# Input projections by Strassen's scheme, as one phase ahead of the attentions

## The chip, the cores and the metric

The kernel runs on one core of a Trainium2 chip. The metric is the device time of one execution in microseconds, the median over runs. TensorE is called PE in the profile (its weight loads PEld), VectorE DVE, ScalarE ACT, GpSimd POOL, and SyncE, which issues the DMAs, SP.

## What is computed

Two layers of a streaming encoder, for 1024 prompt tokens and for 8 streams of 16 sample tokens with caches. In each layer (shortened from the reference):

```python
h = x @ w_in                                    # 1024 -> 2756 columns, split into 11 parts
(c_q, c_kv, k_rope, g_mla, f_q, f_k, f_v, f_logit, g_fox, m_q, g_mem) = split(h)
q   = rms_norm(c_q) @ w_uq                      # 4 heads x (128 + 64 rotated)
lat = rms_norm(c_kv); kr = rope(k_rope)         # outputs of the kernel as well
logf = log_sigmoid(f_logit + b_f)
o_mla = attend(q, [lat @ w_ukv keys, kr], lat @ w_ukv values)   # chunk-causal, 4 heads x 128
o_fox = attend(f_q, f_k, f_v, cumsum(logf))     # causal, with forgetting, 4 heads x 64
o_mem = attend(m_q, mem @ w_mk, mem @ w_mv)     # 256 memory rows, 4 heads x 64
mixed = [o_mla*silu(g_mla), o_fox*silu(g_fox), o_mem*silu(g_mem)]
y = layer_norm(alpha * x + mixed @ w_out)
```

All is float32. A product is carried in a rounded high part and the rest (hi and lo, type fp32r) of both operands, as three matmuls.

## The kernel before

Every product goes through `mm3` (lines 193 to 195, hi by hi, hi by lo, lo by hi), plain products through `mm` (198) and transposes through `tr` (202). `split` makes hi with a cast on ACT (177, 180) and lo with a subtraction on DVE (178, 181); `wsplit` does it for weights, lo on DVE or POOL (187). The token operand X of a layer is feature-major: four blocks of 256 prompt tokens and one of the 128 sample tokens, each in eight chunks of 128 features.

The input projection is cut into eleven groups of columns. `tokproj` gives a token-major result (tokens on partitions, 128 of them, the group's 302 or 306 columns moving), `featproj` a feature-major one (128 columns on partitions, 256 tokens moving); 24 matmuls each, contracted over 1024 features. The groups are the gates `ge`, `gf`, `gm0`, `gm1` (`gates`, silu at 375), the queries `mq`, `fq0`, `fq1` (`qproj`, 353), keys and values of the fox heads `kv0`, `kv1` (`fox_kv`, 523 to 571) and the low-rank rows `lr0`, `lr1` (`lowrank`).

Order within a layer: `ge`, the memory keys and values (`mem_prep`), `mq`; then the memory attention, then the fox attention in two pairs of heads, then `lowrank` with the row norms and its transposes, the queries Q (`mla_x`), rotated queries (`qrope`), the latent attention and the tail (`w_out`, layer norm). `attn` runs one unit of an attention (scores and softmax of 256 queries of a head) and then the P transposes and P times V of the unit before; between units it takes a step of filler generators. In the memory attention the filler is `kv0` and `gf`, in the fox attention `gm` and the sample streams' attention. So the projections stand between softmax steps of the attentions. In layer 0's tail the output tiles are transposed into layer 1's X as they come, and `mem_prep` of layer 1 runs there.

A scheduler orders each engine's instructions by simulated times and priority of the program order. PSUM has three banks `pss`, two `psx`, two `pst` (transposes) and one `pso` (attention outputs); SBUF pools give `u` 25 slots and `w` 8 slots of 4 KB, `x` 12 of 2 KB.

Of the kernel before, what the change touches and what calls it, by code (L numbers as in the profile page):

```python
# [74 lines left out]
RPOOL = (1, 3, 5, 7)
PRE = 9
JF = (2,3,1,0)
JA = (0,2,1,3)
TURN = (3,7)


class Enc:
# [141 lines left out]
    def xpair(self, tiles, banks=None):  # L224

        out = []
        for kh in range(2):
            hi = self.u([P, 4, 256], F32R, "xh")
            lo = self.u([P, 4, 256], F32R, "xl")
            for kk in range(2):  # L230
                ps = (banks or [self.pst])[kk % len(banks or "1")]()
                v = ps.rearrange("p (k t) -> p k t", k=2)
                for a in range(2):
                    for b in range(2):
                        k = kh * 4 + kk * 2 + a
                        self.tr(v[:, a, b * P:(b + 1) * P], tiles[b][:, k * P:(k + 1) * P])
                self.split(hi[:, kk * 2:kk * 2 + 2, :], lo[:, kk * 2:kk * 2 + 2, :], v)
            out.append((hi, lo))
        return out
# [13 lines left out]
    def xtok(self, X, i, k):  # L253

        if i == 8:
            return tuple(t[:, k, :] for t in X[4])
        return tuple(t[:, k % 4, (i % 2) * P:(i % 2 + 1) * P] for t in X[i // 2][k // 4])


    def wload(self, src, alloc=None):  # L260

        parts, _, kn, n = src.shape
        raws = []
        for a in range(parts):
            raw = (alloc or self.w)([P, kn, n if n <= P or n > 256 else 256], name="raw")
            self.load(raw[:, :, :n], src[a])
            raws.append(raw[:, :, :n])
        return raws

    def wprep(self, src, raws=None, pieces=1):  # L270

        out = []
        for raw in raws or self.wload(src):
            _, kn, n = raw.shape
# [3 lines left out]
            for a in range(0, kn, kn // pieces):  # L278
                k = slice(a, a + kn // pieces)
                self.wsplit(hi[:, k, :n], lo[:, k, :n], raw[:, k])  # L280
# [1351 lines left out]
```

## Time and profile before

| | |
|---|---|
| median of 3 runs | 1437.37 us (1436.32 to 1439.52) |
| the profiled execution's own time | 1439.67 us |
| its span in the trace | 1437.9 us |
| PE busy | 1402.4 us, 98% |
| DVE, ACT, POOL busy | 756.6, 620.8, 515.8 us (53%, 43%, 36%) |
| DMA | 180.64 MB, mean 126 GB/s |
| granted clock, mean over the span | 0.99 |

A row of a group reads: line, engine, operation, output<-inputs, shapes, count, then busy time in us and mean ns of one, then the engine's idle time just before these and what ended it. A row of stages reads: stretch in us, its length, busy time and count on each engine, the clock granted to TensorE, DMA share, GB/s. A timeline row reads: start in us, duration, engine, line, operation. Matmuls overlap in the records, so their pace is the distance of their starts.

### The profile page before, as it was taken

The numbers are of one execution on the slowest core, as the hardware profiler recorded it, in microseconds if no ns is written. First come the engines' busy times: TensorE is split into PE (matmuls) and PEld (weight loads), VectorE is DVE, ScalarE is ACT, GpSimd is POOL, SyncE is SP. The second block draws the span as 40 slices with busy tenths as digits, with TensorE's granted clock in tenths as the row PEclk, the third lists the DMA queues.
The fourth block names the chain that finished last, engine by engine and source line by source line (L and its number), as shares of the span: only waits on it lengthen the run. The fifth ranks groups of instructions, "written<-read, shape, count | busy, mean of one in ns | idle before, by whom it ended". The sixth has DMA issues, their size and how long they took to land.

```text
span 1437.9 us, 27746 instructions
## 1 busy us (share of the span) xinstructions
PE 1402.4 (98%) x10222; PEld 1257.8 (87%) x10222; DVE 756.6 (53%) x1863; ACT 620.8 (43%) x1624; POOL 515.8 (36%) x722
## 2 busy tenths in 40 slices
PE   7999999999999999999999999999999999999997
PEld 6999989989988788888899999899899887887885
DVE  6236555266045665666663365643642565566664
ACT  6344454354255544722233454544533554455100
POOL 0233254354364221712322234434625541235121
PEclk9999999999999999999999999999999999999999
DMA  7223332345254431363541234234443633234531
GB/s 286 91 73 91 113 126 87 124 140 166 83 176 130 133 115 53 132 215 118 181 160 54 85 101 153 78 89 137 142 148 113 203 95 123 96 114 143 165 118 73
DMA packets 142344, 180.64 MB, mean 126 GB/s; under 512 B 32384, under 2 KB 99776, under 8 KB 142208
## 3 DMA queue, kind: packets, MB, share of 16 engines
q1 hardware_dynamic: 142208, 178.86, 38.6%
q8 instruction: 81, 1.33, 0.4%
q14 instruction: 55, 0.45, 0.1%
HBM read 138.69 MB, written 40.12 MB: 124 GB/s over the span
## 4 chain that ended last, share of the span: by engine, by line
PE 87%; DMA 4%; DVE 3%; ACT 2%; POOL 2%; issue 1%; SPq 0%; POOLq 0%; DVEq 0%; ACTq 0%
PE pss L193 15%; PE pss L195 14%; PE pss L194 14%; PE pss L198 10%; PE pso L198 7%; PE pst L202 7%; PE psx L198 6%; PE psx L193 4%; PE psx L195 4%; PE psx L194 4%; DMA memx<-in_mem_t_dram 1%; POOL wl L187 1%; PE psx L202 1%; DMA raw<-in_w_uqn_dram 1%; DMA g<-md 1%
## 5 line engine op out<-in xcount | busy, mean ns | idle before, releaser
L187 POOL TENSOR_TENSOR wl<-raw,wh 128x1024 fp32r<-128x1024 f32 (+3 forms) x40 | 101.6, 2543 | 208.1 <-ACT wh L184 98.1
L178 DVE TENSOR_TENSOR ptw<-pst,ptw 128x512 fp32r<-128x512 f32 (+1 forms) x192 | 122.0, 642 | 55.2 <-ACT ptw L177 53.8
L177 ACT CAST ptw<-pst 128x512 fp32r<-128x512 f32 (+1 forms) x192 | 103.4, 552 | 97.3 <-PE pst L202 88.9
L193 PE MATMUL pss<-wh,xh 128*128 128x306 f32 (+1 forms) x384 | 118.2, 309 | 0.4 <-ACT h L693 0.4
L195 PE MATMUL pss<-wh,xl 128*128 128x306 f32 (+1 forms) x384 | 117.6, 307 | 0.0
L194 PE MATMUL pss<-wl,xh 128*128 128x306 f32 (+1 forms) x384 | 117.5, 307 | 0.0
L193 PE MATMUL psx<-xh,wh 128*128 128x256 f32 x384 | 109.9, 287 | 7.8 <-ACT wh L184 6.7
L193 PE MATMUL pss<-woh,msh 128*128 128x512 f32 x288 | 114.0, 396 | 0.7 <-ACT msh L1251 0.6
L195 PE MATMUL pss<-woh,msl 128*128 128x512 f32 x288 | 114.0, 397 | 0.1
L194 PE MATMUL pss<-wol,msh 128*128 128x512 f32 x288 | 113.6, 394 | 0.0
L193 PE MATMUL pss<-xh,wh 128*128 128x256 f32 x384 | 109.9, 286 | 0.2
L194 PE MATMUL psx<-xl,wh 128*128 128x256 f32 x384 | 109.8, 286 | 0.0
L195 PE MATMUL psx<-xh,wl 128*128 128x256 f32 x384 | 108.9, 285 | 0.0
L195 PE MATMUL pss<-xh,wl 128*128 128x256 f32 x384 | 108.4, 282 | 0.0
L194 PE MATMUL pss<-xl,wh 128*128 128x256 f32 x384 | 108.3, 282 | 0.0
L396 POOL TENSOR_SCALAR pa<-pa,col 128x128 f32<-128x128 f32 (+3 forms) x64 | 47.7, 750 | 109.4 <-DVE col L395 62.0
L193 PEld LDWEIGHTS psx<-xh,wh 128*128 128x128 f32 x384 | 73.6, 192 | 8.5 <-ACT wh L184 6.7
L198 PE MATMUL pso<-ptw,vh 128*128 128x256 f32 (+1 forms) x336 | 73.7, 296 | 2.3 <-DVE ptw L178 1.3
L193 PEld LDWEIGHTS pss<-xh,wh 128*128 128x128 f32 x384 | 72.5, 189 | 2.9 <-DVE col L431 1.5
L184 ACT CAST wh<-raw 128x1024 fp32r<-128x1024 f32 (+4 forms) x52 | 54.8, 1057 | 45.7 <-PE pss L194 14.4
L193 PEld LDWEIGHTS pss<-wh,xh 128*128 128x128 f32 x384 | 72.4, 189 | 2.2 <-ACT h L693 1.8
L195 PEld LDWEIGHTS pss<-wh,xl 128*128 128x128 f32 x384 | 72.3, 189 | 1.6 <-issue 1.6
(364 smaller groups left out, 4198.9 us busy)
## 6 DMA issues: line engine op xcount, KB each, us to landing
gd<-gg SPq DMA_DIRECT2D x64, 128.0 KB
kT<-in_fox_kt_dram SPq DMA_DIRECT2D x32, 256.0 KB
vraw<-in_fox_v_dram SPq DMA_DIRECT2D x32, 256.0 KB
kT<-in_mla_kt_dram SPq DMA_DIRECT2D x32, 256.0 KB
vraw<-in_mla_v_dram SPq DMA_DIRECT2D x32, 256.0 KB
raw<-in_w_out_dram SPq DMA_DIRECT2D x16, 512.0 KB
g<-md SPq DMA_DIRECT2D x16, 512.0 KB
raw<-in_w_lr_dram SPq DMA_DIRECT2D x8, 612.0 KB
```

Of the source, the lines that this page charges most:

```text
L177: nc.scalar.copy(hi, ps)
L178: nc.vector.tensor_tensor(lo, ps, self.f(hi), op=ALU.subtract)
L184: self.nc.scalar.copy(hi, raw)
L187: (self.nc.vector if dve else self.nc.gpsimd).tensor_tensor(lo, raw, self.f(hi), op=ALU.subtract)
L193: self.nc.tensor.matmul(ps, ah, bh, start=first and x == 0, stop=False)
L194: self.nc.tensor.matmul(ps, ah, bl, start=False, stop=False)
L195: self.nc.tensor.matmul(ps, al, bh, start=False, stop=last and x == n - 1)
L198: self.nc.tensor.matmul(ps, lhsT, rhs, start=start, stop=stop)
L202: self.nc.tensor.transpose(out, in_, self.ident[:k, :k])
L396: self.nc.gpsimd.tensor_scalar(p, p, rs, 1.0, op0=ALU.mult, op1=ALU.mult)
```

## The change

`w_in` is regrouped ahead of the launch into eleven pairs of 256 columns (2816, with 60 columns of padding), and the whole projection is made by `project()` before any attention. For each pair, tokens and features are each cut in halves and the pair's two chunks of 128 columns are the third split, so that a pair is a 2x2 block product; seven products (Winograd's form, each 12 matmuls of 128x512, into three banks `pss` and two `psx`) take the place of eight. For that, sums of token blocks (`xprep`) are made once per layer, sums of weight blocks (`wsums`) per pair, and sums of the products after it (`u2`, `u3`, `v`, `cout`). The sample tokens take 24 ordinary matmuls of 128x256 per pair (`part`).

```diff
+    def xprep(self, r):                      # operands s1..s4 and 22, per layer
+        for k in range(4):
+            t1, t2 = self.pe(), self.pe()
+            dve.tensor_tensor(t1, r["21"][k], r["22"][k], op=ALU.add)
+            dve.tensor_tensor(t2, t1, r["11"][k], op=ALU.subtract)
+            self.xone(s1, k, t1, dve)        # xone: hi by ACT, lo by the engine named
...
+            pool.tensor_tensor(t4, r["12"][k], t2, op=ALU.subtract)
+            self.xone(s2, k, t2, dve)
...
+            pool.tensor_tensor(t3, r["11"][k], r["21"][k], op=ALU.subtract)
+            self.xone(s3, k, t3, dve)
+            self.xone(s4, k, t4, dve)
+            self.xone(a22, k, r["22"][k], pool)
...
+    def wbase(self, raw):
+        h, l = self.pw([P, 4, 256], F32R, "wh"), self.pw([P, 4, 256], F32R, "wl")
+        self.nc.scalar.copy(h, raw)
+        self.nc.gpsimd.tensor_tensor(l, raw, self.f(h), op=ALU.subtract)
...
+    def wsums(self, raws):
...
+        def one(a, b, op=ALU.subtract):
+            r = self.x([P, 4, P], name="tr")
+            dve.tensor_tensor(r, a, b, op=op)
+            t = self.w([P, 2, 4, P], F32R, "wt")
+            self.nc.scalar.copy(t[:, 0], r)
+            dve.tensor_tensor(t[:, 1], r, self.f(t[:, 0]), op=ALU.subtract)
...
+    def project(self, l, X, XS):
...
+        for n, name in enumerate(PAIRS):
...
+            prod(a, cols(B0, 0), "11")
+            p1 = self.pe()
+            nc.scalar.copy(p1, a)
...
+            part(sm, B0, 0)
+            part(sm, B1, 1)
...
+            prod(a, cols(B1, 0), "12")
+            self.cout(name, 0, 0, a, p1)
...
+            prod(d, T[0], "s1")
...
+            prod(b, T[1], "s2")
+            u2 = self.pe()
+            nc.vector.tensor_tensor(u2, b, p1, op=ALU.add)
+            v = self.x([P, 512], name="co")
+            nc.gpsimd.tensor_tensor(v, u2, p5, op=ALU.add)
...
+            prod(c, T[2], "s3")
+            u3 = self.pe()
+            nc.vector.tensor_tensor(u3, c, u2, op=ALU.add)
+            self.cout(name, 1, 1, p5, u3)
...
+            prod(d, cols(B1, 1), "s4")
+            self.cout(name, 1, 0, d, v, v)
...
+            prod(c, T[3], "22")
+            self.cout(name, 0, 1, c, u3)
```

All results are feature-major and go to DRAM: gates, after their silu on 128x512 tiles, to `gd` as before, the rest to fourteen chunks `cd`. The attentions reload them: `qhead` (mem and fox query heads, 128x1024), `fox_kv` (keys doubled on the partitions, values by transposes), `early_rows` (rotary key and forget logits, by transposes) and `lowrank`. The norms of the prompt's low-rank rows are now over partitions:

```diff
+            nc.scalar.activation(q, t, AF.Square)                 # 5 chunks of 128x1024
...
+            for c in (slice(0, 512), slice(512, D)):
+                ps = self.psw()
+                self.mm(ps, self.ones, q[:, c])
+                nc.vector.tensor_scalar(r[:, c], ps, 1.0 / n, EPS, op0=ALU.mult, op1=ALU.add)
+                nc.gpsimd.tensor_tensor(r[:, c], r[:, c], self.mhalf.broadcast_to([P, 512]), op=ALU.pow)
...
+            nc.vector.scalar_tensor_tensor(t, t, self.ng[:, c:c + 1], rs[0 if kv else 1], op0=ALU.mult, op1=ALU.mult)
...
+            hi, lo = self.u([P, D], F32R, "lrh"), self.u([P, D], F32R, "lrl")
+            nc.scalar.copy(hi, t)
+            nc.gpsimd.tensor_tensor(lo, t, self.f(hi), op=ALU.subtract)
```

The filler of the memory and fox attentions is now `proj()`: `fox_kv`, Q of the four heads, `qrope`, the first V and K of the latent attention; the sample streams run beside both. `mem_prep` of layer 1 is no longer in layer 0's tail. The tail takes its tiles in the order 0 to 5, 8, 6, 7, and behind tile 7 comes `xprep` of layer 1. Pools: `u` 30 slots, `w` 4. The outputs `p_lat`, `p_fk` and `p_fv` are written feature-major and turned round after the launch.

How it moves instructions. POOL, from the memory values to the memory attention's softmax, before (`mv` are memory values, `wl` weight rests, `pm` the memory softmax's rows):

```order
L338 TENSOR_TENSOR mv_335<-st_485,mv_335 128x4x64
L187 TENSOR_TENSOR wl_671<-raw_664,wh_670 128x1024
L187 TENSOR_TENSOR wl_971<-raw_966,wh_970 128x1224
L509 TENSOR_SCALAR pm_952<-pm_952,col_962 128x256 x2
L509 TENSOR_SCALAR pm_1027<-pm_1027,col_1037 128x256 x2
```

and after (`rs` are the norms' factors, `lrl` the rests of the normed low-rank rows):

```order
L499 TENSOR_TENSOR mv_2393<-st_2571,mv_2393 128x4x64
...
L851 TENSOR_TENSOR rs_2640<-rs_2640,mhalf 128x512 x2
...
L851 TENSOR_TENSOR rs_2658<-rs_2658,mhalf 128x512 x2
...
L862 TENSOR_TENSOR lrl_2791<-lr_2365,lrh_2790 128x1024
L862 TENSOR_TENSOR lrl_2797<-lr_2367,lrh_2796 128x1024
...
L862 TENSOR_TENSOR lrl_2802<-lr_2369,lrh_2801 128x1024
...
L862 TENSOR_TENSOR lrl_2807<-lr_2371,lrh_2806 128x1024
L746 TENSOR_TENSOR lex_2743<-lex_2743,lf_2722 128x4
L862 TENSOR_TENSOR lrl_2812<-lr_2373,lrh_2811 128x1024
L643 TENSOR_SCALAR pm_2816<-pm_2816,col_2826 128x256 x2
```

The powers and the subtractions of the low-rank rows, which stood behind the attentions, are now in POOL's queue ahead of the first scaling of a memory softmax row. DVE at the same place, after (`lr` are the low-rank rows, `pss` under `TENSOR_REDUCE` the memory scores):

```order
L850 TENSOR_SCALAR rs_2658<-pss_2663 128x512
...
L857 SCALAR_TENSOR_TENSOR lr_2365<-lr_2365,ng_297,rs_2640 128x1024
L857 SCALAR_TENSOR_TENSOR lr_2367<-lr_2367,ng_297,rs_2640 128x1024
L857 SCALAR_TENSOR_TENSOR lr_2369<-lr_2369,ng_297,rs_2658 128x1024
...
L637 TENSOR_REDUCE col_2817<-pss_2815 128x2
L641 RECIPROCAL col_2826<-col_2818 128x2
L666 TENSOR_TENSOR fkl_2999<-fkr_2995,fkh_2998 128x1024
```

The products of the norms stand ahead of the first maximum of memory scores. PE in the memory attention, before (`kd` doubled fox keys, `wh_970` weights of `kv0`, `ptw` split P tiles):

```order
L194 MATMUL psx_1407<-wl_971,xh_492 128x306
L198 MATMUL pso_1226<-ptw_1232,mv_334 64x256
L198 MATMUL pso_1226<-ptw_1232,mv_335 64x256
L198 MATMUL pso_1226<-ptw_1232,mv_335 128x256
L202 MATMUL pst_1299<-ident,pm_1173 128x128 x4
L195 MATMUL psx_1407<-wh_970,xl_493 128x306
L193 MATMUL psx_1407<-wh_970,xh_492 128x306
```

and after:

```order
L187 MATMUL pst_2875<-ident,pm_2816 128x128 x4
L183 MATMUL pss_3148<-mkh_2389,q_2493 128x256
L183 MATMUL pss_3148<-mkl_2391,q_2493 128x256
...
L187 MATMUL pst_2915<-ident,pm_2837 128x128 x4
L183 MATMUL pso_2874<-ptw_2880,mv_2392 128x256
L187 MATMUL psx_3368<-ident,spr_3290 128x128 x2
L183 MATMUL pso_2874<-ptw_2880,mv_2392 64x256
L183 MATMUL pso_2874<-ptw_2880,mv_2393 64x256
```

Between two P transposes there stood projection matmuls on tokens X; now scores and sample work stand there.

More of the change, by code (lines that the diff above doesn't have):

```diff
@@ L221, in late_consts, with xop @@
         self.load(self.sin, self.i["k_sin"])
[L224 to L239, printed above, removed]
+    def xop(self):
+        return [(self.u([P, 2, 512], F32R, "xh"), self.u([P, 2, 512], F32R, "xl")) for _ in range(2)]
@@ L251, in xsample @@
         return hi, lo
[L253 to L267, printed above, removed]
-        return raws
@@ L284, in tokproj, with wraw @@
[L284 to L289 removed]
+    def wraw(self, l, n):
+        raws = [self.ptw([P, 4, 256], F32, "raw") for _ in range(2)]
+        for a in range(2):
+            self.load(raws[a], self.i["w_pairs"][l, n, a])
+        return raws
@@ L292, in mem_prep, with wprep @@
+    def wprep(self, raws):
+        out = []
+        for raw in raws:
+            hi, lo = self.w(raw.shape, F32R, "wh"), self.w(raw.shape, F32R, "wl")
+            self.wsplit(hi, lo, raw)
+            out += [(hi[:, k], lo[:, k]) for k in range(raw.shape[1])]
+        return out
     def mem_prep(self, l):
@@ L301, in mem_prep, with raws @@
                 M.append((hi, lo))
-        alloc = lambda shape, name: self.ptw(shape, F32, name)
-        raws = self.wload(self.i["w_mk"][l], alloc)
+        def raws(src):
+            out = []
+            for a in range(2):
+                raw = self.ptw([P, 4, 256], F32, "raw")
+                self.load(raw, src[a])
+                out.append(raw)
+            return out
+        W = self.wprep(raws(self.i["w_mk"][l]))
         yield
@@ new lines, in fox_kv @@
+        K = []
+        for e in range(2):
+            t = self.w([P, D], name="fkr")
+            self.twice(6 + p, e, t)
+            hi, lo = self.u([P, D], F32R, "fkh"), self.u([P, D], F32R, "fkl")
+            nc.scalar.copy(hi, t)
+            nc.vector.tensor_tensor(lo, t, self.f(hi), op=ALU.subtract)
+            K.append((hi, lo))
+            yield
+        t = self.u([P, D], name="fvr")
+        self.load(t, self.cd[8 + p])
+        V = [self.x([P, 2, 2, P], F32R, "fv") for _ in range(4)]
@@ L570, in fox_kv @@
+        for g in range(2):
+            pt = self.pst()
+            for a in range(4):
+                kb = g * 4 + a
+                self.tr(pt[:, a * P:(a + 1) * P], t[:, kb * P:(kb + 1) * P])
+            for b in range(2):
+                src = pt[:, b * 256:b * 256 + 256].rearrange("p (k e d) -> p k e d", k=2, e=2)
+                v = V[g * 2 + b]
+                self.split(v[:, :, :, 0:64], v[:, :, :, 64:128], src)
             yield
-        self.fkv = KH, KL, V
+        self.fkv = K, V
@@ L1257, in tail_start, with tail @@
         return lg, lb, prep
-    def tail(self, WO, start, ready, after, fill, early):
+    def tail(self, WO, start, ready, after, fill):
         nc = self.nc
@@ L1449, in fill @@
                 next(sg, None)
-        if not start:
-            start.extend(self.tail_start(l, xin))
-        self.tail(WO, start, ready, after, fill, early)
+        start.extend(self.tail_start(l, xin))
+        self.tail(WO, start, ready, after, fill)
     def main(self):
@@ L1476, in more @@
[L1476 to L1494 removed]
+        nc = self.nc
```

824 lines of the change are left out of this document (394 added, 430 removed).

## The prediction

> **What bounds the kernel now.** I read the share of each engine and the chain of waits first, then busy time by stage, then the groups of instructions by shape, and last single rows of the timeline for paces.
>
> ```profile
> PE 1402.4 (98%) x10222; PEld 1257.8 (87%) x10222; DVE 756.6 (53%) x1863; ACT 620.8 (43%) x1624; POOL 515.8 (36%) x722
> PE 87%; DMA 4%; DVE 3%; ACT 2%; POOL 2%; issue 1%; SPq 0%; POOLq 0%; DVEq 0%; ACTq 0%
> ```
>
> TensorE is busy 98% of the span and is 87% of the chain, so a matmul taken away is worth its time, as long as nothing new makes TensorE wait. By stage (length, then busy time of PE, PEld, DVE, ACT, POOL, then clock, DMA share, GB/s):
>
> ```profile
> 0.00:10.00 10.00, 3.30 (x15) 3.30 (x16) 4.20 (x7) 5.71 (x9) 0.43 (x6) 1.00 0.80 297
> 10.00:20.00 10.00, 9.71 (x75) 9.51 (x74) 8.75 (x15) 7.71 (x14) 0.00 (x0) 1.00 0.90 336
> 20.00:36.00 16.00, 12.21 (x82) 10.91 (x82) 11.12 (x17) 9.84 (x18) 0.00 (x0) 0.89 0.66 247
> 84.00:175.00 91.00, 88.69 (x692) 86.78 (x691) 46.63 (x112) 45.10 (x134) 31.75 (x50) 0.98 0.34 98
> 175.00:353.00 178.00, 176.67 (x1493) 165.33 (x1491) 94.67 (x277) 87.10 (x219) 89.25 (x126) 1.00 0.42 128
> 353.00:411.00 58.00, 57.51 (x467) 54.71 (x466) 11.29 (x36) 19.75 (x70) 25.20 (x40) 1.00 0.37 114
> 411.00:482.00 71.00, 70.35 (x543) 58.77 (x542) 41.90 (x106) 38.95 (x112) 29.07 (x59) 1.00 0.47 145
> 482.00:614.00 132.00, 130.08 (x873) 106.88 (x872) 80.23 (x237) 68.68 (x182) 47.69 (x46) 1.00 0.33 113
> 614.00:735.00 121.00, 120.34 (x600) 99.84 (x601) 75.16 (x109) 25.77 (x38) 28.03 (x26) 1.00 0.51 174
> 735.00:745.00 10.00, 9.59 (x81) 9.30 (x80) 7.85 (x11) 4.33 (x7) 3.87 (x3) 1.00 0.39 118
> ```
>
> These are layer 0's start, memory attention (84 to 175), fox attention (to 353), low-rank projection (to 411), turns and queries (to 482), latent attention (to 614) and tail; 735 opens layer 1. TensorE waits only in the first 36 us. Elsewhere DVE and POOL are about half busy, and projection matmuls stand between softmax steps as cover.
>
> **Matmuls removed and added.** Pace is the distance of starts, since ends overlap; between each pair of rows are 24 steps.
>
> ```profile
> 757.34 0.28 PE L193 MATMUL psx<-wh,xsh 128*128 128x256 f32 x1
> ...
> 760.17 0.28 PE L193 MATMUL psx<-xh,wh 128*128 128x256 f32 x1
> ...
> 359.72 0.30 PE L193 MATMUL pss<-wh,xh 128*128 128x306 f32 x1
> ...
> 363.12 0.30 PE L193 MATMUL pss<-wh,xh 128*128 128x306 f32 x1
> ...
> 1399.80 0.40 PE L193 MATMUL pss<-woh,msh 128*128 128x512 f32 x1
> ...
> 1405.45 0.40 PE L193 MATMUL pss<-woh,msh 128*128 128x512 f32 x1
> ```
>
> That is 2.83/24 = 0.118 us at 256 columns, 3.40/24 = 0.142 at 306, 5.65/24 = 0.235 at 512. The code before issues for both layers' input projections 2544 matmuls of 256 columns, 1296 of 306, 432 of 302 and 96 of 128: 300 + 184 + 60 + 6 = about 545 us, taking the last two in proportion. After, each of 22 pairs has 7 x 12 of 512 columns and 24 of 256: 19.8 + 2.8 = 22.6 us, in all 497; with the fill of the weight loads I take 251 a layer, 502. Not an eighth is saved but 43 us, because padding adds 60 columns to 2756.
>
> **What each pair asks of the others.** Weight sums: 8 DVE subtractions on 128x512; output sums: 5 on DVE from PSUM, 2 on POOL; two weight splits on POOL.
>
> ```profile
> L178 DVE TENSOR_TENSOR xl<-x,xh 128x512 fp32r<-128x512 f32 x16 | 10.2, 687 | 5.8 <-ACT xh L177 5.7
> L187 POOL TENSOR_TENSOR wl<-raw,wh 128x1024 fp32r<-128x1024 f32 x22 | 52.6, 2400 | 82.3 <-ACT wh L184 45.4 <-PE psx L194 18.6 <-ACT ggt L382 9.5
> L187 POOL TENSOR_TENSOR wv<-raw,wv 128x512 fp32r<-128x512 f32 x4 | 5.2, 1299 | 15.1 <-ACT wv L184 11.4 <-PE pss L195 3.7
> L187 DVE TENSOR_TENSOR wl<-raw,wh 128x1024 fp32r<-128x1024 f32 x8 | 9.8, 1224 | 4.2 <-ACT wh L184 3.3 <-PE psx L194 0.7
> L184 ACT CAST wh<-raw 128x1024 fp32r<-128x1024 f32 x30 | 31.5, 1051 | 31.5 <-PE pss L194 11.8 <-POOL wl L187 5.6 <-DMA raw<-in_w_gf_dram 3.6
> ```
>
> DVE 13 x 0.69 = 8.9 us, POOL 2 x 2.4 + 2 x 1.3 = 7.4. Even one after the other that is 16.3 under 22.6 of TensorE (a gate pair has four more DVE products, 20 in all), so the pairs cost nothing beside the matmuls. Stores and reloads of the projected rows add 7.3 MB each way per layer on SP's queue; with weights and gates about 23 MB fall in 251 us, 92 GB/s against the 336 that the second stage row carried.
>
> **Start and turn of layers.** Before, the first matmuls needed one split block. Now the seven token operands need DVE 36 operations of 0.69 (25 us) and POOL 2 x 2.4 + 16 x 1.3 = 26. They may exclude each other:
>
> ```profile
> 345.92 2.83 POOL L187 TENSOR_TENSOR wl<-raw,wh 128x1224 fp32r<-128x1224 f32 x1
> ...
> 346.33 2.73 DVE L702 TENSOR_TENSOR kr<-early,cos 128x288 f32<-128x288 f32 x1
> 348.99 0.45 DVE L703 TENSOR_TENSOR kr<-early,sin 128x288 f32<-128x288 f32 x1
> ```
>
> L702 and L703 are the same size; the one that began beside a POOL subtraction ended 0.3 us after that did, 2.3 late. Taken so, 51 us of preparation begin near 6 us, pair 0 ends near 60 and TensorE has 22 us of work in it: 38 idle, against about 21 side by side. At the turn before, no gap shows (9.59 of 10). Now the last tail tile's layer norm (7) stands ahead of 16 POOL operations and 24 DVE ones, 21 + 16.5, and weights: 45 us in which TensorE has half a pair's products: 31 idle, or 14 side by side.
>
> **The bridge.** Attention can start only behind reloads, norms and memory keys. TensorE has some 27 us of work there (keys and values of memory, transposes, sample queries), the chain is longer: memory weights (load, cast 1.05, split 2.4, two products) and reload of rows to about 20 us; four sums of squares and their DVE scaling to 23; then four powers of 128x512 on POOL, five DVE products of 1.22, the first two alone ahead of a cast, five POOL subtractions of 2.4. The memory softmax's POOL scaling is queued behind those subtractions and its DVE reductions behind the products; the P transposes on TensorE wait for both. The power on a wide tile is nowhere in the trace:
>
> ```profile
> L673 POOL TENSOR_TENSOR col<-col,mhalf 128x1 f32<-128x1 f32 x36 | 19.8, 551 | 2.2
> L728 POOL TENSOR_TENSOR col<-col 128x1 f32<-128x1 f32 x18 | 3.5, 196 | 1.3 <-ACT jk L727 1.1
> ```
>
> A power of one column takes 551 ns, an addition 196. Low end: as a plain operation of 512 columns, 1.30 us. High end: all 355 ns extra recur per column, 182 us. I take the ratio of these two rows, 2.8 x 1.30 = 3.6 us, nearest to the low end, since that row has the size. Then the chain is 23 + 4 x 3.6 + 2 x 1.2 + 1 + 5 x 2.4 = 53 us, and some 2 more with exclusion: 55 a layer. Each us of the power adds 4 a layer, 8 in all.
>
> By the Trainium skill, GPSIMD Engine Reference, 2.1 and 3.1, GpSimd runs an elementwise operation as a software loop, with about 2.6 cycles per element and 12 more where it branches on data; if the power branches once, 512 x 12 / 1.2 GHz gives an estimated 5.1 us above a plain operation, 6.4 each, and the total would be 22 us above mine. No run shows it yet.
>
> **Memory and fox attention.** DVE 46.6 + 94.7 = 141 us now.
>
> ```profile
> L353 DVE SCALAR_TENSOR_TENSOR qf<-pss,qf 64x256 fp32r<-64x256 f32 x32 | 13.5, 422 | 26.5 <-ACT qf L352 26.5
> L181 DVE SCALAR_TENSOR_TENSOR qr<-pst,qr 64x256 fp32r<-64x256 f32 x32 | 13.4, 422 | 7.6 <-ACT qr L180 6.9
> L375 DVE SCALAR_TENSOR_TENSOR gg<-gg,pss 128x256 f32<-128x256 f32 x32 | 13.4, 418 | 6.2 <-ACT gg L374 5.7
> L178 DVE TENSOR_TENSOR vl<-pss,vh 128x256 fp32r<-128x256 f32 x32 | 13.1, 420 | 4.6 <-ACT vh L177 4.2
> L569 DVE TENSOR_TENSOR fkl<-pst,fkh 128x256 fp32r<-128x256 f32 x32 | 12.4, 419 | 21.3 <-ACT fkh L567 21.2
> L178 DVE TENSOR_TENSOR xnl<-pss,xnh 128x512 fp32r<-128x512 f32 x16 | 11.0, 690 | 8.7 <-ACT xnh L177 8.6
> L558 DVE CAST fv<-st 128x128 fp32r<-128x128 f32 x32 | 7.2, 229 | 50.8 <-ACT st L554 50.2
> ```
>
> Per layer go: keys 6.2, values 3.6, fox queries 6.75, 26 gate products of 0.418, 10.9. Come: wide keys and heads 8 x 1.22, value splits 8 x 0.42, Q 8 x 0.69, rotated queries 16 x 0.42, V 8 x 0.42, K 2 x 0.69: 30. With small rotations, near 148. TensorE: 269 less the projections that leave (432 of 302 to 306, 840 of 256, 48 of 128: 163) less 4 of transposes, plus 35 of Q, V and K moved in (84 of 512, 120 of 256, transposes): 137. DVE becomes the bound, late next is its subtraction of each P tile. At nine tenths density (full is 148, eight tenths 185) 165 us replace 269. Latent attention and tail stay: 264 and 224 for two (the memory preparation, 11, leaves the first tail). The 58 and 71 us stages end: their projections are in the pairs, Q in the stretch, the rest in the bridge.
>
> **Sum.** 38 + 502 + 2 x 55 + 2 x 165 + 264 + 224 + 31 = 1499, some 4 less for work that overlaps the seams: 1495. The profiled execution, 1439.67, is 1.8 above its span and 2.3 above the median; these cancel.
>
> **Rivals.** (a) Faster. DVE carries bridge and stretch as one dense stream: its work in the bridge is some 31, so 31 + 148 = 179 a layer instead of 220, total 1413 to 1420. For it: 51% and 53% busy DVE now has idle to fill, and filler for TensorE exists; against it: POOL's power, five subtractions and the softmax scaling are one queue. It decides from bridge plus stretch under 190 a layer. (b) The power costs per column: 15 us makes 8 x 11.4 = 91 more, 1586; 22 us, 1642; the high end, about 2900. For it is 551 against 196 at one column. (c) DVE and POOL run side by side in the preparations: 17 + 17 and 10 in the bridges, 1451. Rows of DVE reading PSUM show no delay; L702 speaks against. (d) The clock. From 20 to 36 us, TensorE busy 76%, the granted clock was 0.89. If the stretch ran at half clock, TensorE would need 274 instead of 165, 1713. The Trainium skill, TensorE: Matmul & The Clock Gate, Part 1, says that an idle window of about 3.4 us halves the clock; by it, my three gaps would cost a few us, while the stretch's waits, a few tenths each, would not trip it; the 0.98 at 84 to 175 fits. That the matmuls don't shrink is hardly possible, 7506 against 9586 being issued.
>
> **Chances.** My forecast 0.43 (own range 1465 to 1540); (a) 0.17; (b) up to 22 us 0.22, above 0.09; (c) 0.07; (d) 0.02. A range of 1425 to 1640 leaves out half of (a) and the powers above 22 us. Faster by over 0.2% (what three runs can tell): most of (a) and a little of (c), 0.17; within it 0.04; slower 0.79.
>
> **What the changed profile would show.** Pairs at 22.6 us each with TensorE full; a gap of about 38 at the start and 31 at the turn; POOL's powers near 3.6 us; DVE operations with two SBUF inputs stretched beside POOL subtractions; about 28 idle TensorE in each bridge; DVE near 90% in the stretch. Pairs above 25 us, or powers of tens of us, would break the sum from above; a bridge under 35 from below.

## The result, and the profile after

The changed kernel takes 2219.1 us (median of 4, 2216.6 to 2219.67), the kernel before beside it 1438.44: a ratio of 1.5421, 95% interval 1.5387 to 1.5454. The forecast was 1495, its range 1425 to 1640. The page of the changed kernel, engines, slices, chain, and the first groups of instructions by line:

```profile
span 2217.4 us, 23907 instructions
PE 1395.9 (63%) x8150; PEld 1143.0 (52%) x8150; DVE 991.6 (45%) x2050; ACT 671.1 (30%) x1524; POOL 1285.1 (58%) x689
PE   5999960000018779999879999610000087799998
POOL 5433269999993654131264332599999936541421
PEclk7999985555559889999989999855555588899999
PE 34%; POOL 13%; issue 5%; DVE 4%; DMA 3%; ACT 2%; SPq 0%; POOLq 0%; DVEq 0%; ACTq 0%
L851 POOL TENSOR_TENSOR rs<-rs,mhalf 128x512 f32<-128x512 f32 x8 | 656.3, 82048 | 0.0
L857 DVE SCALAR_TENSOR_TENSOR lr<-lr,ng,rs 128x1024 f32<-128x1024 f32 x10 | 16.9, 1742 | 605.1 <-POOL rs L851 605.1
```

TensorE is idle in two blocks, in each of which POOL is full. The group row says with what: eight powers of 82.0 us each, 656 us in all, and DVE's norm products waited 605 us for them. POOL gained 769 us of busy time, all but 113 of it there. The chain view names POOL for 13% only; its shares add up to 61% of the span, so the slices and the group row are the better guide here.

By stage of the changed kernel: the start and the pairs of layer 0, the bridge up to the powers, the powers, the rest of the bridge, memory attention and fox attention; behind the dots the turn of the layers and the pairs of layer 1 (columns as before: length, busy PE, PEld, DVE, ACT, POOL, clock, DMA share, GB/s):

```profile
11.40:65.00 53.60, 38.66 (x115) 26.01 (x116) 44.26 (x39) 21.14 (x35) 38.81 (x22) 0.75 0.24 85
65.00:285.60 220.60, 220.57 (x1093) 186.82 (x1092) 99.23 (x149) 79.58 (x133) 78.12 (x50) 1.00 0.41 140
285.60:317.40 31.80, 21.87 (x138) 19.68 (x139) 21.39 (x41) 14.02 (x27) 11.85 (x11) 0.84 0.57 161
317.40:646.30 328.90, 9.80 (x65) 6.71 (x64) 9.66 (x23) 7.74 (x23) 328.90 (x7) 0.52 0.06 16
646.30:673.60 27.30, 14.76 (x90) 9.23 (x91) 19.19 (x28) 13.52 (x40) 24.80 (x27) 0.56 0.26 80
673.60:727.00 53.40, 46.88 (x309) 38.07 (x308) 40.04 (x87) 34.90 (x100) 19.52 (x32) 0.89 0.55 151
727.00:872.20 145.20, 114.80 (x905) 88.86 (x906) 104.50 (x313) 78.94 (x194) 82.48 (x137) 0.91 0.48 144
...
1121.50:1137.00 15.50, 11.85 (x64) 9.58 (x62) 13.12 (x22) 5.28 (x14) 9.79 (x6) 0.89 0.09 35
1137.00:1167.00 30.00, 17.84 (x50) 11.98 (x51) 25.90 (x27) 14.67 (x25) 20.44 (x11) 0.70 0.10 35
1167.00:1394.00 227.00, 226.95 (x1110) 191.71 (x1109) 101.97 (x153) 79.22 (x133) 82.36 (x52) 0.99 0.40 137
```

The pairs do what was forecast: TensorE is full in them (220.57 of 220.60), and the first matmuls on sample tokens of two pairs that follow each other start 22.2 us apart:

```profile
243.72 0.28 PE L178 MATMUL pst<-wh,xsh 128*128 128x256 f32 x1
...
265.91 0.28 PE L178 MATMUL pst<-wh,xsh 128*128 128x256 f32 x1
```

The four powers of the first bridge follow one another through 328.9 us in which TensorE does 9.8 us of work at a clock of 0.52.

The forecast's terms beside the same stretches of the span, both layers together:

| | forecast, us | measured, us |
|---|---|---|
| start and pairs, layer 0 | 38 + 251 = 289 | 285.6 |
| bridges | 110 (28.8 of it powers) | 388.0 + 390.0 = 778.0 (656.3 powers) |
| memory and fox attention | 330 | 198.6 + 195.2 = 393.8 |
| latent attention and tails | 488 | 249.3 + 238.2 = 487.5 |
| turn and pairs, layer 1 | 31 + 251 = 282 | 272.5 |
| sum | 1499 | 2217.4 |

Of the 718 that are missing, 627 are the powers' price, 41 the rest of the bridges, 64 the two stretches; the other terms came out 13 us shorter together.

### The profile page after: what moved, and what is told of

Its sections match the earlier page's. It is cut to its first block, busy times and chain, and to the rows that moved or that the text cites. A ratio compares the mean times of both kernels' runs of the same rounds, so it can differ in the third digit from the quotient of the medians.

```text
span 2217.4 us, 23907 instructions
## 1 busy us (share of the span) xinstructions
PE 1395.9 (63%) x8150; PEld 1143.0 (52%) x8150; DVE 991.6 (45%) x2050; ACT 671.1 (30%) x1524; POOL 1285.1 (58%) x689
## 4 chain that ended last, share of the span: by engine, by line
PE 34%; POOL 13%; issue 5%; DVE 4%; DMA 3%; ACT 2%; SPq 0%; POOLq 0%; DVEq 0%; ACTq 0%
POOL rs L851 11%; PE pss L178 6%; PE pss L180 6%; PE pss L179 6%; PE pss L183 4%; PE pso L183 3%; PE pst L187 2%; PE psx L183 2%; PE psx L178 1%; PE psx L179 1%; PE psx L180 1%; DMA sck<-cumd 1%; DMA qraw<-cd 0%; DVE xl L223 0%; DVE ptw L163 0%
## 5 line engine op out<-in xcount | busy, mean ns | idle before, releaser
L851 POOL TENSOR_TENSOR rs<-rs,mhalf 128x512 f32<-128x512 f32 x8 | 656.3, 82048 | 0.0
L857 DVE SCALAR_TENSOR_TENSOR lr<-lr,ng,rs 128x1024 f32<-128x1024 f32 x10 | 16.9, 1742 | 605.1 <-POOL rs L851 605.1
L187 PE MATMUL psx<-ident,spr 128*128 128x128 f32 x96 | 16.8, 298 | 315.4 <-POOL spr L530 315.3
L274 POOL TENSOR_TENSOR wl<-raw,wh 128x1024 fp32r<-128x1024 f32 x44 | 105.9, 2407 | 153.4 <-ACT wh L273 85.7
L179 PE MATMUL pss<-xl,wt 128*128 128x512 f32 x264 | 105.4, 399 | 6.6 <-DVE xl L223 6.6
L178 PE MATMUL pss<-xh,wt 128*128 128x512 f32 x264 | 105.5, 400 | 4.9 <-ACT xh L222 4.9
L180 PE MATMUL pss<-xh,wt 128*128 128x512 f32 x264 | 105.2, 398 | 1.0 <-DVE wt L288 1.0
L287 ACT CAST wt<-tr 128x512 fp32r<-128x512 f32 x88 | 54.2, 621 | 157.1 <-DVE tr L285 152.3
L340 POOL TENSOR_TENSOR co<-pe,pe 128x512 f32<-128x512 f32 x22 | 28.3, 1287 | 89.0 <-issue 51.3
L530 POOL TENSOR_SCALAR pf<-pf,col 128x640 f32<-128x640 f32 (+3 forms) x64 | 49.7, 778 | 50.3 <-DVE col L529 50.3
L178 PE MATMUL pss<-xh,wh 128*128 128x512 f32 x176 | 71.3, 405 | 11.4 <-ACT wh L273 11.4
```

The source lines that it names most:

```text
L178: self.nc.tensor.matmul(ps, ah, bh, start=first and x == 0, stop=False)
L179: self.nc.tensor.matmul(ps, ah, bl, start=False, stop=False)
L180: self.nc.tensor.matmul(ps, al, bh, start=False, stop=last and x == n - 1)
L187: self.nc.tensor.transpose(out, in_, self.ident[:k, :k])
L274: self.nc.gpsimd.tensor_tensor(l, raw, self.f(h), op=ALU.subtract)
L287: self.nc.scalar.copy(t[:, 0], r)
```

## The experiments

**Is the power the whole of it?** Multiplications of the same size in its place (the norms are then not computed):

```diff
-                nc.gpsimd.tensor_tensor(r[:, c], r[:, c], self.mhalf.broadcast_to([P, 512]), op=ALU.pow)
+                nc.gpsimd.tensor_tensor(r[:, c], r[:, c], self.mhalf.broadcast_to([P, 512]), op=ALU.mult)
```

> The changed kernel with the four powers per layer on 128x512 replaced by multiplications of the same size on the same queue (the norms are then not computed; nothing else differs). Theory A, the powers alone are the miss: the sum of the prediction with 1.3 us in place of 3.6 each, 1495 - 8 x 2.3 = 1477 us. Theory B, the powers are 8 x (82.0 - 1.3) = 646 us of it and some 90 us lie elsewhere (the stretch of memory and fox attention was 198 and 195 us where 165 was forecast, the bridge without powers 59 where 41 was): 2217 - 646 = about 1570 us. Rival C, work that now hides under the powers comes back behind them (PE 10 to 14, DVE 10 to 12 us per layer): 1590 to 1600 us.

Measured 1593.08 us (1587.1 to 1596.86). Theory A falls: with the powers gone the kernel is still 1.1075 times the kernel before (1.1042 to 1.1108). Theory B with rival C fits: without the powers the time is 626 us less (2219.1 to 1593.08) while the eight themselves became 648 shorter (82.0 each against 1.04 for a multiplication), so some 22 us of work that had run beside them show again.

**What a power costs.** Extra operations in the kernel before, ahead of its work:

```diff
+        for n in (8, 32, 64, 128):
+            nc.gpsimd.tensor_tensor(wq[:, 0:n], wq[:, 0:n], self.mhalf.broadcast_to([P, n]), op=ALU.pow)
+        nc.gpsimd.tensor_tensor(wq[0:64, 0:64], wq[0:64, 0:64], self.mhalf[0:64].broadcast_to([64, 64]), op=ALU.pow)
+        nc.gpsimd.tensor_tensor(wq, wq, self.mhalf.broadcast_to([P, 128]), op=ALU.mult)
```

> The kernel before with six extra GpSimd operations ahead of its work: powers of 128x8, 128x32, 128x64, 128x128 and 64x64, and a multiplication of 128x128. If the price is per column, 0.160 us each above 0.39: 1.7, 5.5, 10.6 and 20.9 us, and 10.6 for the 64 partitions too; if it is per element over all partitions, the 64x64 takes half of the 128x64; if it is a fixed price or a cliff at large sizes, the small ones stay near 0.55. The multiplication: 0.47 us.

The groups by shape of that run:

```profile
L218 POOL TENSOR_TENSOR wq<-wq,mhalf 128x128 f32<-128x128 f32 x1 | 20.7, 20727 | 0.1
L218 POOL TENSOR_TENSOR wq<-wq,mhalf 128x64 f32<-128x64 f32 x1 | 10.5, 10521 | 0.1
L219 POOL TENSOR_TENSOR wq<-wq,mhalf 64x64 f32<-64x64 f32 x1 | 10.5, 10509 | 0.0
L218 POOL TENSOR_TENSOR wq<-wq,mhalf 128x32 f32<-128x32 f32 x1 | 5.4, 5429 | 0.1
L218 POOL TENSOR_TENSOR wq<-wq,mhalf 128x8 f32<-128x8 f32 x1 | 1.7, 1659 | 0.1
L220 POOL TENSOR_TENSOR wq<-wq,mhalf 128x128 f32<-128x128 f32 x1 | 0.4, 394 | 0.0
```

(20.727 - 10.521) / 64 = 0.159 us per column. The one-column row from before (0.551) less that leaves 0.39 besides, and the two give 82 for 512 columns, as measured, and the other widths within 0.3 us. Half the partitions cost the same (10.509 for 64x64, 10.521 for 128x64). So the price is per column, with no cliff.

**The same norms with a narrow power.** Tokens on partitions, one power of 128x16 per layer, spread again through ones times diagonal tiles:

```diff
+                self.mm(ps[:, a * 8 + i:a * 8 + i + 1], q[:, i * P:(i + 1) * P], self.ones[:, 0:1])
...
+        nc.gpsimd.tensor_tensor(ss, ss, self.mhalf.broadcast_to([P, 16]), op=ALU.pow)
...
+                    nc.scalar.activation(dg, self.ident, AF.Copy, scale=ss[:, k:k + 1])
+                    self.mm(ps[:, i * P:(i + 1) * P], self.ones, dg)
```

> The changed kernel with the same norms, but the power taken on one 128x16 tile per layer (tokens on partitions: 16 matmuls of one column for the sums), and spread over partitions by 16 matmuls of ones with diagonal tiles and four ACT copies. The power at 0.16 us a column: 16 x 0.16 + 0.39 = 3.0 us; the spreading some 8 us of chain (16 ACT scalings of 128x128 at 0.3, then copies), so 6 us per layer above the run with multiplications (4 x 1.3): about 12 us above that one, 1585 us by theory B, 1489 by theory A.

Measured 1585.29 us (1582.0 to 1587.92). That is theory B's number, but in part by luck: 12 us above the run with multiplications were forecast, and it came out 8 below it, with bridges 5 and 7 us shorter (68.9 and 69.3 in place of 74.0 and 76.4); why is not known. The rest of the miss was to be found in this kernel.

**Do DVE and GpSimd exclude each other?** The forecast had taken so for the start. In the changed kernel, POOL's and then DVE's timeline there:

```profile
18.41 6.81 POOL L223 TENSOR_TENSOR xl<-xr,xh 128x512 fp32r<-128x512 f32 x4
25.19 1.72 POOL L247 TENSOR_TENSOR pe<-xr,xr 128x512 f32<-128x512 f32 x1
```

```profile
22.34 1.76 DVE L285 TENSOR_TENSOR tr<-raw 128x512 f32<-128x512 f32 x1
24.03 1.75 DVE L223 TENSOR_TENSOR xl<-pe,xh 128x512 fp32r<-128x512 f32 x1
...
27.38 0.68 DVE L285 TENSOR_TENSOR tr<-raw,tr 128x512 f32<-128x512 f32 x1
```

POOL's four take 1.70 each instead of 1.3, and DVE's beside them 1.76; at 27.38, with POOL idle, 0.68. Both start 1.7 us apart there, so one of each takes 1.7 us, where one after the other would be 1.98 and side by side 1.3: nearly exclusion. The sixteen block operations per layer that the forecast counted for POOL were then given to DVE:

```diff
-            pool.tensor_tensor(t4, r["12"][k], t2, op=ALU.subtract)
+            dve.tensor_tensor(t4, r["12"][k], t2, op=ALU.subtract)
...
-            self.xone(a22, k, r["22"][k], pool)
+            self.xone(a22, k, r["22"][k], dve)
```

> As the run with the narrow power, and the 16 GpSimd operations on token blocks per layer (sums t3, t4, the low parts of blocks 12 and 22) moved to DVE. If two-input operations of DVE and GpSimd exclude each other, 16 x 1.3 to 1.8 us of GpSimd become 16 x 0.69 = 11 us of DVE: about 10 us less at the start and 8 less at the turn of the layers, some 18 us faster than the run beside it. If they run side by side, DVE alone becomes the chain: 52 x 0.69 = 36 against 25 us, some 10 to 20 us slower.

Measured 1572.3 us (1569.47 to 1574.13) against 1585.29: 13 faster, on the side of exclusion, 5 less than forecast. The runs that follow are edits of this kernel unless said.

**Seven products or eight?** In the kernel with the narrow power:

```diff
-            prod(d, T[0], "s1")
...
+                    prod(a, cols(B0, c), f"{h + 1}1", True, False)
+                    prod(a, cols(B1, c), f"{h + 1}2", False, True)
+                    self.cout(name, c, h, a)
```

> As the run with the narrow power (1585 us), with eight ordinary block products per pair in place of seven (24 matmuls accumulate in one bank, no sums of blocks before or after), in the same phase ahead of the attentions. TensorE gets 12 more matmuls of 0.235 us for each of 22 pairs, 62 us; the start needs only one split block at a time (28 us of idle less) and the turn of the layers only the last blocks (12 to 18 less). So 1600 to 1608 us: the scheme of seven products by itself gains some 20 us, and the phase in front costs some 165. Rival, the sums of blocks also hold up the pairs: below 1585, the scheme gains nothing.

Measured 1590.26 us (1585.98 to 1592.05) against 1585.29 (1582.0 to 1587.92): the ranges overlap, so a gain of 5 us from the scheme is not clear of noise. A pair takes 24.9 us where seven products take 22.2, so 60 us are saved in the pairs. The pace of two pairs with eight, then the whole stretch up to the end of layer 0's pairs, with seven and with eight:

```profile
229.34 0.28 PE L179 MATMUL pst<-wl,xsh 128*128 128x256 f32 x1
...
254.26 0.28 PE L179 MATMUL pst<-wl,xsh 128*128 128x256 f32 x1
```

```profile
0.00:285.80 285.80, 258.39 (x1207) 212.67 (x1207) 148.05 (x191) 105.24 (x174) 118.00 (x78) 0.96 0.39 136
```

```profile
0.00:292.80 292.80, 277.45 (x1339) 233.48 (x1339) 65.62 (x77) 65.31 (x101) 79.99 (x50) 1.00 0.41 141
```

With seven, TensorE is idle 27 us there and its clock 0.96; with eight 15 us, at 1.00, and no gap is left at the turn of the layers. So only 7 us of layer 0's 30 remain at the end of its pairs, and 9 in layer 1: 44 of the 60 go in the start and the turn. Another 13 go in the bridges, which are 62.4 and 62.7 us with eight and 68.9 and 69.3 with seven. Eight products were not run with the preparation on DVE.

**Bridge and stretch.** From the end of the pairs to the first P transposes of the memory attention was 73 us in the run of 1572, memory and fox attention 200; forecast 41 without powers and 165. Of the bridge TensorE is busy 50.5 us, at a clock of 0.77:

```profile
274.00:347.00 73.00, 50.51 (x307) 43.51 (x307) 46.25 (x75) 38.15 (x95) 35.85 (x34) 0.77 0.54 158
```

Three edits on the bridge. First, the low parts of the normed rows on DVE. POOL and DVE at that place, one group of consecutive operations each:

```profile
326.55 12.22 POOL L874 TENSOR_TENSOR lrl<-lr,lrh 128x1024 fp32r<-128x1024 f32 x4 [9.12 <-ACT lrh L873]
```

```profile
326.99 9.57 DVE L869 SCALAR_TENSOR_TENSOR lr<-lr,ng,rs 128x1024 f32<-128x1024 f32 x3 [1.88 <-ACT rs L863]
```

DVE's three took 3.19 us each, 1.22 alone.

```diff
-            nc.gpsimd.tensor_tensor(lo, t, self.f(hi), op=ALU.subtract)
+            nc.vector.tensor_tensor(lo, t, self.f(hi), op=ALU.subtract)
```

> As the run with the preparation on DVE (1572 us), and the five low parts of the normed low-rank rows (128x1024) per layer taken from GpSimd to DVE. In that run three DVE products (1.22 alone) and four GpSimd subtractions (2.4 alone) took 12.2 us together, one after the other. If they exclude each other, DVE alone needs 10 x 1.22 = 12.2 us in all in place of 2.5 + 12.2 + 2.4 = 17: 5 us less per layer, about 1562. If the bridge is set by the order of TensorE's work ahead of it, 0 to 3 us in all.

Measured 1570.47 us (1566.12 to 1575.36), no difference from 1572.3, though in the profiled runs the bridges fell from 73 to 62 and from 70 to 63 us: the stretch grew from 200 to 205, in layer 1 from 205 to 211.

Second, the norms' sums and products ahead of the memory keys in program order:

```diff
         next(mp)
+        for _ in range(3):
+            next(lr)
+        drain(lr)
         QM = [self.qhead(10, 0, S64)]
```

> As the run with the preparation on DVE (1572 us), but the sums, the power and the products of the low-rank norms stand in program order ahead of the memory keys and values and the sample queries, not behind them. Theory O, the bridge (73 us there, 55 forecast) is long because the norm sums wait behind other TensorE work though their squares were summed 35 us before: the products then run beside the memory keys, the first memory softmax starts 15 to 25 us earlier in each layer, total 1525 to 1545. Rival, the memory weights' chain (load, cast, split, two products one after the other) sets the bridge anyway: 5 to 10 us in all.

Measured 1573.61 us (1571.02 to 1575.15): nothing. POOL's low parts now end at 309 us in place of 343, the first P transposes still come at 348. Theory O falls: behind the norms the rotary keys, forget gates and sample queries stand ahead of the memory scores.

Third, with the norms first as in the run before, these too were taken out of the bridge and made filler of the memory attention:

```diff
+        def pre():
+            next(er)
+            yield
...
+            ncq.append(self.forget(l))
+            yield
+            self.s_cum(l)
```

> As the run with the preparation on DVE (1572 us), with the norms first in program order, and the rotary keys, the forget gates and the sample queries taken from the bridge into the memory attention as filler (one step per unit, ahead of the fox keys). In all runs so far bridge and stretch together took 267 to 275 us a layer, whichever of the two was shortened. If the bridge is long because that work is done with TensorE idle between its steps, it is now spread over softmax steps that leave TensorE idle too: 15 to 25 us less a layer, 1525 to 1540. If bridge plus stretch is fixed by the amount of work on TensorE and its clock (214 us busy of 273, clock about 0.88) the sum stays at 270 a layer: 1565 to 1575.

Measured 1587.76 us (1583.29 to 1590.42), 15 slower. The bridge did fall, from 73 to 58 us, and the stretch rose from 200 to 218. With layer 1's memory keys at the turn of the layers as well:

```diff
+        if l:
+            drain0 = [x for x in self.mem_prep(l)]
         self.project(l, X, XS)
```

> As the run before it, with layer 1's memory keys and values made ahead of its projection, at the turn of the layers where TensorE is idle some 20 us (as the kernel before has them in layer 0's tail), and 13 slots of 2 KB in place of 12. Its 11 us of TensorE then fall into idle time and leave layer 1's bridge: 10 to 15 us less than the run beside it. If the six slots that they hold through the projection starve the sums of products there, the pairs of layer 1 get longer than 22.7 us and the gain is gone.

Measured 1596.78 us (1594.87 to 1602.16), slower again: layer 1's bridge fell to 46 us, but its pairs ended 25 us later.

**What holds the stretch?** Five single causes, each in a run or two.

The sample streams, taken out of the memory attention, and out of both:

```diff
-PERM = 1
+PERM = 0
```

> As the run with the preparation on DVE (1572 us), but the sample streams' attention is not stepped in the memory attention (as in the kernel before), only from the fox attention on. If the stretch of memory and fox attention (200 us, 36 of them TensorE idle) is long for the sample's loads and its small chained steps, the memory part gets shorter by some 10 us a layer and the work comes back on TensorE later, where TensorE has idle: 1555 to 1572. If those steps were cover for the softmax chain, the time rises, 1575 to 1595.

> As the run with the preparation on DVE (1572 us), with the sample streams' attention stepped neither in the memory nor in the fox attention; it comes in the latent attention and the tail, where TensorE is busy 98 and 93%. If the sample's loads and small chained steps hold up the stretch, memory and fox attention fall from 200 to 160 to 175 us a layer and the work returns later at its TensorE price (some 20 us a layer), total 1535 to 1570. If they ran in idle time for nothing, the stretch stays near 190 and the total rises to 1600 to 1640 (leaving them out of the memory attention alone gave 25 more).

Measured 1597.09 us (1592.73 to 1599.5), 2 above the upper forecast, and, with PERF = 0 too, 1640.4 (1636.13 to 1641.5). The three parts of the first stretch in the second run:

```profile
346.90:390.40 43.50, 39.70 (x244) 34.26 (x242) 36.78 (x79) 35.30 (x97) 16.62 (x31) 0.98 0.34 95
390.40:414.40 24.00, 16.44 (x93) 13.60 (x92) 19.74 (x53) 11.27 (x27) 16.38 (x29) 0.86 0.22 58
414.40:532.10 117.70, 91.05 (x680) 71.45 (x681) 83.76 (x244) 66.55 (x167) 61.69 (x107) 0.88 0.45 131
```

It takes 185 us in place of 200, its TensorE 147 in place of 164, and what follows it grows by 65 and 33 us in the two layers. It is not free of sample work: the scheduler draws steps forward, and the trace has 186 matmuls of the sample streams in it, as many as the memory and fox attention of the kernel before (425 in the run of 1572). So the steps cost 15 us a layer where they stand, nearly their 17 of TensorE, and 33 to 65 behind it: they are cheapest here, but little of them falls into idle time.

A second unit in flight (`LAGM = 2`, `LAGF = 2`), alone and with the low parts on DVE:

> As the run with the preparation on DVE (1572 us), with the P transposes and P times V of a unit two units behind its scores in the memory and fox attentions, not one. In the stretch there no engine is full (TensorE 82%, DVE 75%). If its length is set by the softmax chain of a unit (scores, maximum, exponential, scaling, transposes, split) for lack of independent work behind it, a second unit in flight fills it: 10 to 25 us less a layer, 1520 to 1550. If DVE's work is the bound after all, or TensorE at its lowered clock, nothing changes: 1565 to 1575.

> As the run beside it, and with the five low parts of the normed rows on DVE (which took 11 us from the first bridge, but nothing from the total). If the second unit in flight lifts what holds the stretch, those 7 to 11 us a layer now reach the total: 10 to 20 us below the run beside it. If bridge and stretch together stay near 270 us a layer, the two runs are alike within 5 us.

Measured 1575.58 us (1571.99 to 1578.27), no gain: the softmax chain of one unit isn't what holds it. The second, 1565.48 (1562.5 to 1570.15), is 10 below it, at the edge of the forecast; it is the fastest that keeps the whole computation, 1.0874 times the kernel before (1.0849 to 1.0899), though the low parts on DVE alone (1.0908, 1.0880 to 1.0936) are not clearly slower.

The filler, taken out and made in one piece behind:

```diff
-        attn(memu(), LAGM, (pj, 1), (sg, PERM))
+        attn(memu(), LAGM, (pj, 0), (sg, PERM))
```

> As the run with the preparation on DVE (1572 us), with Q, the rotated queries, V and K of the latent attention (35 us of TensorE a layer) not stepped into the memory and fox attention but made at once behind them (only the first fox keys and values are made ahead). If they are cover for softmax chains, the stretch stays near 190 and a stage of 35 to 45 us follows: 1620 to 1650. If each of their steps holds the attention up as long as it takes (in-order queues, DVE and ACT shared), the stretch falls by about as much, and the total stays within 15 us.

Measured 1571.4 us (1567.81 to 1578.23). The three parts of the stretch and the stage behind it:

```profile
344.70:387.80 43.10, 33.88 (x255) 26.46 (x253) 34.02 (x84) 30.18 (x99) 16.02 (x34) 0.90 0.54 153
387.80:404.10 16.30, 10.57 (x41) 7.08 (x41) 15.43 (x32) 10.19 (x20) 9.64 (x12) 0.60 0.83 220
404.10:518.40 114.30, 98.37 (x760) 74.02 (x759) 78.99 (x235) 60.59 (x147) 66.13 (x101) 0.91 0.54 159
518.40:552.90 34.50, 33.13 (x226) 27.25 (x225) 25.36 (x70) 17.51 (x49) 14.59 (x29) 1.00 0.31 92
```

The first stretch falls to 174 us and a stage of 34 follows, in which TensorE is busy 33.1. So Q, V and K cost 27 us inside the attention and 34 alone: they find little idle time there.

The clock, held up by matmuls whose results are overwritten:

```diff
                 po = self.pso()
+                for _ in range(8):
+                    self.mm(po, KH[0][:, 0, 0:P], KH[0][:, 0, :])
```

> As the run with the preparation on DVE (1572 us), with eight matmuls of 128x256 more per unit of the memory and fox attentions (32 units a layer), whose results are overwritten; they stand ahead of each unit's P times V, 0.94 us a unit at full clock, 30 us a layer. If the lowered clock (0.93, 0.80, 0.93 in the three parts of the stretch) is what lengthens it, they hold it at 1.00 and cost at most 10 us a layer, or gain: 1550 to 1590. If TensorE's own time is the bound they cost 30 us a layer, 1632; if TensorE has idle time in every unit, and neither clock nor TensorE bounds, 1572 to 1590 with the clock little changed.

Measured 1606.23 us (1604.09 to 1613.29). The three parts of the stretch, in the kernel with the preparation on DVE and then in this one:

```profile
347.10:402.30 55.20, 48.61 (x349) 38.90 (x348) 44.05 (x99) 38.33 (x115) 22.76 (x39) 0.93 0.60 168
402.30:431.60 29.30, 23.35 (x206) 19.27 (x206) 22.32 (x67) 13.85 (x35) 21.21 (x36) 0.79 0.61 190
431.60:547.40 115.80, 91.89 (x703) 70.29 (x701) 83.17 (x246) 65.23 (x160) 62.11 (x102) 0.94 0.45 132
```

```profile
351.30:415.40 64.10, 60.29 (x478) 50.95 (x478) 46.70 (x108) 38.97 (x118) 24.86 (x44) 0.98 0.49 147
415.40:439.30 23.90, 19.75 (x185) 16.18 (x183) 19.20 (x54) 12.63 (x33) 16.56 (x26) 0.99 0.53 156
439.30:566.70 127.40, 108.23 (x850) 87.67 (x848) 86.91 (x253) 66.40 (x161) 64.59 (x108) 0.92 0.46 136
```

The stretch is 215 us, 15 longer, for 30 us of matmuls: half of them went into idle time, half did not, between the two forecasts. In the first two parts the clock is at 0.98 and 0.99, and they take 88.0 us in place of 84.5: there the lowered clock is not what holds the stretch. In the third part, more than half of it, the clock was not raised (0.92 for 0.94), so for that part the run does not tell.

Last, DVE, relieved of the subtraction that makes the low part of each P tile there:

```diff
-            self.split(pt[:, 0, :c], pt[:, 1, :c], ps[:, :c])
+                self.nc.scalar.copy(pt[:, 0, :c], ps[:, :c])
...
-        h, l = pt[:, 0, cs], pt[:, 1, cs]
+        h, l = pt[:, 0, cs], self.zl[:, cs]
```

> As the run with the preparation on DVE (1572 us), without DVE's subtraction that makes the low part of each transposed P tile in the memory and fox attentions (56 of 0.55 to 0.69 us a layer, some 36 us of DVE; their matmuls run on a constant zero tile, so that TensorE's work is the same and the products lack the low parts of P). If DVE, busy 75% with the chains through it, sets the stretch (200 us a layer), it falls by 20 to 35 us a layer: 1505 to 1535. If DVE is not what holds it, the stretch stays above 190: 1555 to 1572.

Measured 1561.53 us (1557.67 to 1564.46), 11 less. The same three parts of this run:

```profile
348.10:401.10 53.00, 49.00 (x347) 38.32 (x347) 35.22 (x84) 37.57 (x113) 21.92 (x39) 0.92 0.60 175
401.10:427.00 25.90, 20.47 (x167) 16.00 (x165) 19.70 (x60) 12.53 (x31) 20.09 (x32) 0.90 0.59 172
427.00:544.30 117.30, 93.77 (x743) 76.18 (x744) 65.06 (x215) 67.14 (x164) 64.24 (x107) 0.89 0.49 143
```

DVE falls from 149.5 to 120.0 us busy and TensorE's stays (163.9, 163.2); the first stretch is 4 us shorter, 196 for 200. DVE by itself was not the bound.

## Why the prediction was wrong

**The power.** The step that failed is the price of a power of 128x512. The forecast had put bounds of 1.30 and 182 us, and took 3.6, the ratio of the one-column rows times the plain wide row, because that row "has the size". The size was the wrong likeness: the operation is what repeats per column, and the one-column row can't tell its fixed part (0.39) from its part per column (0.159). Two bounds a factor of 140 apart on a term with a weight of 8 should have widened the range to the upper one; the upper rival, priced at about 2900, had 0.09. Its mechanism (the price recurs per column) is what happened, at less than half of that price. With 82.0 in the forecast's own formula, 1495 + 8 x 78.4 = 2122, still 97 below the measured time: the bridge and the stretch are the second miss.

By the Trainium skill, GPSIMD Engine Reference, 2.1 and 3.1, an elementwise operation is a software loop on GpSimd, and that agrees with the rows; its 12 cycles for a branch, from which the forecast estimated 6.4 us, do not come near the 0.159 us a column that the widths showed.

**The clock** went to 0.52 in the long idle of the bridges and to 0.75 in the start, as rival (d) had it for gaps. In the bridges it cost little because TensorE had little to do. In the start it cost some 15 us, by estimate: the 115 matmuls of the first stage row were busy 38.7 us, and at the pace of 0.227 us that 512 columns have in the pairs, and 0.118 for 256, they would need 23. The forecast had also expected that waits of a few tenths would leave the clock alone. In the start they did not: from 33.0 to 36.4 us no gap of TensorE is longer than 0.95 us, but it is busy 45%, and behind that the clock is halved for 20 us:

```profile
33.00:36.40 3.40, 1.54 (x4) 0.86 (x5) 2.72 (x4) 1.76 (x3) 2.41 (x2) 0.99 0.07 29
36.40:56.80 20.40, 14.20 (x40) 9.26 (x39) 19.58 (x18) 10.70 (x17) 12.99 (x8) 0.50 0.04 13
```

That the clock does not hold up the first two parts of the stretch is shown by the run with matmuls added; for the third part it is not shown.

**The pairs** were right: 22.2 us measured, 22.6 forecast, TensorE full. The four terms of the projections before add up to 550 us, not 545, so 48 us were to be saved and not 43, and the pages of the profile count 10222 and 8150 matmuls where the forecast says 9586 and 7506; the forecast's sum uses none of these.

**Start and turn** were right in their times: pairs of layer 0 end at 285.6 (289 forecast), turn and pairs of layer 1 take 272.5 (282 forecast). In the start that is partly luck: TensorE was idle 26 us there (11.4 and 53.6 less 38.7), not 38, and the lowered clock, which its sum had left out, made up for it. Exclusion of DVE and POOL, taken there over rival (c), holds by the rows at 22 to 28 us and by the 13 us from moving POOL's part to DVE. The Trainium skill, SBUF — State Buffer, Who interferes with whom, says that a DVE instruction with two SBUF inputs contends with a GpSimd instruction that reads SBUF, and calls the shared ports an exclusive lock. The rows agree in the main (0.68 us alone, 1.76 beside), but a pair took 1.70, less than the 1.98 of the two one after the other.

**The bridge** without powers was forecast as 41, and is 59 in the changed kernel (388.0 - 328.9) and 74 with multiplications: the 27 us put down for TensorE were 50.5 busy at a clock of 0.77 in the run of 1572. Two causes named in the forecast, the queue behind the norms and the subtractions of POOL, are not it: taking either away moved nothing in the total, though the second shortened the bridges by 11 and 7 us.

**The stretch** failed in its bound. DVE's work was right (148 forecast, 144.5 and 149.5 measured), but DVE busy 73 to 75% isn't nine tenths, and with a fifth of its work gone the stretch lost only 4 us. TensorE's share was wrong: 137 forecast, 162 to 164 busy. With as many sample matmuls in it as before (the run with PERF = 0) it is 147, so some 17 of that are steps that now begin in the memory attention and that the forecast had not counted as moved; the other 10 are, by subtraction, put down to the lowered clock, which no run measured by itself. The remaining 36 are idle, in some 10 gaps of over 0.9 us and many small ones, the longest 8 to 11 us at the change of head pairs, where the second pair's keys, bias row and sample loads come on one queue. In the run of 1572:

```profile
494.35 0.64 PE L183 MATMUL psx<-vraw,spr 128*32 128x128 f32 x4 [9.92 <-DMA vraw<-in_fox_v_dram]
```

That gap alone does not explain the stretch: in the first stretch of the run without the filler no gap is longer than 3.8 us, and TensorE is still idle 31 us of 174.

**Rival (a)**, one dense stream, would have needed bridge and stretch under 190 us a layer; with the power out of the way they took 258 to 291 (245 in the run without the filler, with a stage of 34 behind), and of ten edits to their inside none took more than 7 us off the total, apart from the one that leaves work out (11). What fixes that sum stays open: not the power, not one unit's softmax chain, not DVE, not missing filler, and not the clock in the first two parts, as far as single edits show. Several causes at once were edited only in the runs of 1565, 1588 and 1597, and a version in which pairs are interleaved with the attentions again was not built, since the operands of the pairs fill the slots that the attentions need; it is the rival that stands untested.

## What to carry to other kernels

A price that the trace shows for one column says nothing of a wide tile until a second width is measured; if the term is multiplied, take the upper bound into the range. Where a scheme saves matmuls on the full engine, count what its sums cost where that engine waits for them: here 60 us saved in the pairs left some 5, not clear of noise. When work is taken out from between the softmax steps of an attention, expect idle time there: TensorE was idle 4 us of 269 in memory and fox attention before, 37 of 199 after, and the small steps put in its place did not fill it. That the removal is the cause is argued, not shown.

## What the runs showed of the hardware

- A power on GpSimd cost 0.39 us and 0.159 per column (8 to 512 columns), the same on 64 and 128 partitions; a multiplication of 128x128 there took 0.394 us.
- With TensorE 3% busy the granted clock was 0.52. In the start of the changed kernel it was 0.50 from 25 to 29 us, and matmuls of 512 columns started 0.43 us apart there (25.40, 25.83, 26.25), 0.23 in the pairs. Short waits were enough to halve it: 3.4 us with TensorE 45% busy and no gap above 0.95 us.
- DVE operations with two inputs in SBUF and GpSimd operations that met each took nearly the time of both: 1.76 and 1.70 us in place of 0.68 and 1.30.
